# A hybrid decoder trunk: four of eight depthwise-convolution chunks as polyphase products, and a layer norm whose sums come as columns

## The chip, the cores and the metric

The kernel runs on one core of a Trainium2 chip. The metric is the device time of one execution in microseconds (us), the median of repeated runs. One execution is also recorded by the hardware profiler; its engines are PE (TensorE, the matrix engine, with its weight loads as PEld), DVE (VectorE), ACT (ScalarE), POOL (GpSimd) and SP, which here only issues transfers.

## The reference

Two layers over 512 tokens of 1024 features in float32. Layer 0 is a causal Conformer convolution, layer 1 differential attention; each is followed by a SwiGLU feed-forward network and a gated per-layer embedding. Only the convolution module is touched:

```python
def conformer_conv(x, w_pw1, b_pw1, dw_w, dw_b, ln_g, ln_b, w_pw2, b_pw2):
    a = x @ w_pw1 + b_pw1
    u = a[..., :D_MODEL] * jax.nn.sigmoid(a[..., D_MODEL:])
    u = depthwise_causal_conv(u, dw_w, width=31) + dw_b
    u = jax.nn.silu(layer_norm(u, ln_g, ln_b))     # mean and variance over the 1024 features
    return u @ w_pw2 + b_pw2
```

(The call of the convolution is shortened here; it has one filter of 31 taps for each feature.)

## The kernel before

Activations lie transposed: 128 features on the partitions and 512 tokens along a row, so that 1024 features are eight chunks. Every large product is done in three passes (`mm3`, L153) on a split of both operands into a rounded part `hi` and a rest `lo`: a weight tile of 128x1024 is loaded by SP (L146), rounded by ACT (L149), and its rest is taken by DVE (L150) or, for three tiles of the second pointwise layer, by POOL.

The convolution module runs over the eight chunks in one loop (L444 to L485). Iteration c loads the weights of chunk c+1, does the two products `half` of chunk c (gate and value, 24 matmuls each), hands the chunk before to PE's share of the convolution (`pe_taps`), gates chunk c (L462 and L467 scale, L463 is the sigmoid, L479 or L471 multiplies), finishes the chunk before (`other_taps`), and adds an earlier chunk to the running sums of the layer norm (`moments`).

The 31 taps of a chunk are shared out. In a plain chunk PE takes `PE_TAPS[c]` taps as products with diagonal matrices (L306), ACT and POOL take `POOL_TAPS[c]` (ACT multiplies, L390, POOL adds, L391), and DVE the rest, one instruction of 128x512 each (L402). DVE accumulates in a PSUM bank `sc`, except for chunk 7 (`ALONE`), where it accumulates in SBUF (`B7`) and adds PE's bank at L404; L405 adds POOL's part. A chunk in `PHASED` is done by PE alone: the gated chunk is written phase by phase (L471), stored to DRAM (`pi`, L317) and read back with four phases of 32 features on the partitions (L321). Then 4 x 9 products of 128x128x128 (L354) with matrices that hold the taps do the whole convolution. ACT copies the result (L362), it goes to DRAM (`po`, L364) and back (L367), and DVE adds the bias and orders it (L372). The nine matrix tiles of a polyphase chunk, 256 KB each, are loaded by SP into five of the six buffers `D0` to `D5` and into the two buffers of `C5`.

Before the layer norm a per-token shift, the mean over chunk 0, is taken off every chunk: by L424 for chunks below `SHIFT`, as a product of one row into PSUM (L311, L312) for later plain chunks, and inside L372 for polyphase chunks. The squares (ACT, L434) and the chunks are summed by POOL (L436, L438). For the last chunk, products with a matrix of ones put both sums on all partitions (L441, L442); eight DVE instructions (L495) read the diagonals to get them as columns, and L499 to L501 make the reciprocal deviation, which a product spreads over the partitions. `drow`, the mean, is added to all chunks (DVE L507, POOL L509), and a planned loop (L530 to L535) makes the split operands `z` of the second pointwise layer.

The order of each engine's instructions is made when the kernel is built, by a scheduler that plays the program on its own timeline; `issue_after` orders one instruction behind another, and the projections of the embedding (L524) are ordered behind the last tap or the last moment in that way. An engine's queue, SP's too, is in order.

Of the kernel before, what the change touches and what calls it, by code (L numbers as in the profile page):

```python
# [15 lines left out]
ALU = mybir.AluOpType  # L16
# [4 lines left out]
P = 128  # L21
S = 512
D = 1024
NC = D // P
# [21 lines left out]
NV = _at  # L46


SHIFT = 2
WARM = 9  # L50
ZW = 3
ALONE = (7,)
CUTS = 2


PE_TAPS = (0, 4, 0, 0, 0, 0, 0, 14)
POOL_TAPS = (9, 10, 0, 11, 0, 11, 0, 7)


PHASED = (2, 4, 6)  # L60
NPH = 4
FG = P // NPH
LAGS = (KW + NPH - 2) // NPH + 1
LEAD = LAGS - 1
TAPS = []
# [19 lines left out]
def trunk(ctx, tc, xT, pT, wts, diag, dww, vec, rel, onehot, lamv, out):  # L85
    nc = tc.nc
    V, A, G, T = nc.vector, nc.scalar, nc.gpsimd, nc.tensor
# [7 lines left out]
    def sb(shape, tag, bufs, dt=F32):  # L95
        uid[0] += 1
        return pool.tile(shape, dt, tag=tag, name=f"{tag}_{uid[0]}", bufs=bufs)
# [7 lines left out]
    tp = lambda: ps("tp", 2)  # L105
    wk = lambda dt=F32, shape=(P, S): sb(list(shape), "wk", 4, dt)
    big = lambda dt=F32, shape=(P, S): sb(list(shape), "big", 5, dt)
    f = lambda ap: ap.bitcast(F32)
# [10 lines left out]
    ident = sb([P, P], "ident", 1)  # L119
# [173 lines left out]
    def pe_taps(c):  # L293

        acc = accs[c] = sc() if c < NC - 2 else mm()
        if c in PHASED:
            return phased_taps(c, acc)
        if not PE_TAPS[c] and c < SHIFT:
            return
        for j in range(PE_TAPS[c]):  # L300
            if j % 4 == 0:
                n = min(4, PE_TAPS[c] - j)
                dg = sb([P, 4, P], f"D{TAPS.index((c, j)) % 6}", 1)
                with after_weights(c):
                    nc.sync.dma_start(dg[:, :n], diag[TAPS.index((c, j)), :, :n])
            last_tap[0] = T.matmul(  # L306
                acc, dg[:, j % 4], ups[c][:, j : j + S],
                start=(j == 0), stop=(j == PE_TAPS[c] - 1 and c < SHIFT),
            )
        if c >= SHIFT:  # L310
            T.matmul(acc, ones_r[0:1, :], shift[0], start=not PE_TAPS[c], stop=False)  # L311
            last_tap[0] = T.matmul(acc, ones_r[0:1, :], shift[1], start=False, stop=True)  # L312

    def phased_in(c, src):

        d = dram.tile([P, S], F32, tag=f"pi{c}", name=f"pi{c}")
        nc.sync.dma_start(d, src)  # L317
        xs = ups[c] = sb([P, NPH, LEAD + P], f"C{c // 2 % 2}", 2)
        G.memset(xs[:, :, :LEAD], 0.0)
        for i in range(NPH):  # L320
            nc.sync.dma_start(  # L321
                xs[i * FG : (i + 1) * FG, :, LEAD:],
                bass.AP(d.tensor, d.offset + i * P, [[S, FG], [FG * S, NPH], [1, P]]),
            )
# [34 lines left out]
    def phased_out(c):  # L359

        o = big()
        A.copy(o, accs[c])  # L362
        d = dram.tile([P, S], F32, tag=f"po{c}", name=f"po{c}")
        nc.sync.dma_start(d, o)  # L364
        both_ = sb([P, 2, S], f"B{c}", 1)
        for g in range(NPH):
            nc.sync.dma_start(  # L367
                both_[g * FG : (g + 1) * FG, 1].rearrange("p (r n) -> p r n", r=NPH),
                bass.AP(d.tensor, d.offset + g * P, [[S, FG], [FG * S, NPH], [1, P]]),
            )  # L370
        tok = "p (n r) -> p n r"
        V.scalar_tensor_tensor(  # L372
            both_[:, 0].rearrange(tok, r=NPH), both_[:, 1].rearrange("p (r n) -> p n r", r=NPH), col("dw_b", c),
            shrow.rearrange(tok, r=NPH), ALU.add, ALU.add,
        )
        y.append(both_[:, 0])

    def other_taps(c):
        if c in PHASED:
            return phased_out(c)  # L380
        up, acc = ups[c], accs[c]
        tap = lambda j: up[:, j : j + S]
        a, b = PE_TAPS[c], PE_TAPS[c] + POOL_TAPS[c]
        pacc = wk()
        for j in range(a, b):
            if j == a:
                A.activation(pacc, tap(j), AF.Identity, scale=wt(c, j), bias=col("dw_b", c))
            else:
                pr = sb([P, S], f"C{2 + j % 2}", 2)
                A.activation(pr, tap(j), AF.Copy, scale=wt(c, j))  # L390
                G.tensor_tensor(pacc, pacc, pr, ALU.add)  # L391
        yc = sb([P, 2, S], f"B{c}", 1)
        if c == 1:
            sums["acc"] = yc[:, 1]
        yc = yc[:, 0]
        alone = c in ALONE
        sum_ = yc if alone else acc
        if alone or (not a and c < SHIFT):
            V.tensor_scalar(sum_, tap(b), wt(c, b), None, ALU.mult)
            b += 1  # L400
        for j in range(b, KW):
            V.scalar_tensor_tensor(sum_, tap(j), wt(c, j), sum_, ALU.mult, ALU.add)  # L402
        if alone and a:
            V.tensor_tensor(yc, yc, acc, ALU.add)  # L404
        V.tensor_tensor(yc, sum_, pacc, ALU.add)  # L405
        y.append(yc)
# [9 lines left out]
    def moments(c):  # L416
        if c == 0:
            t = sums["first"] = tp()
            T.matmul(t, ones, y[0], start=True, stop=True)
            A.activation(shift[0], t[0:1, :], AF.Copy, scale=-1.0 / P)  # L420
            A.activation(shrow, t, AF.Copy, scale=-1.0 / P)
            V.scalar_tensor_tensor(shift[1], t[0:1, :], -1.0 / P, f(shift[0]), ALU.mult, ALU.subtract)
        if c < SHIFT:
            V.scalar_tensor_tensor(y[c], sums["first"], -1.0 / P, y[c], ALU.mult, ALU.add)  # L424
        if c < SHIFT - 1:
            return
        for i in range(SHIFT) if c == SHIFT - 1 else (c,):
            if i == NC - 1:
                sums["mean"], sums["sq"] = tp(), tp()
            if i == 0:  # L430
                A.activation(sums["acc"], y[0], AF.Square)
                continue
            sq = wk()
            A.activation(sq, y[i], AF.Square)  # L434
            if i < NC - 1:
                G.tensor_tensor(sums["acc"], sums["acc"], sq, ALU.add)  # L436
                if i > 1:
                    G.tensor_tensor(macc, y[1] if i == 2 else macc, y[i], ALU.add)  # L438
                continue
            for n, part, one in (("mean", macc, y[i]), ("sq", sums["acc"], sq)):  # L440
                T.matmul(sums[n], ones, part, start=True, stop=False)  # L441
                last_moment[0] = T.matmul(sums[n], ones, one, start=False, stop=True)  # L442

    for c in range(NC):  # L444
        wa, wg = pairs[c]
        if c == 0:
            pg = half(wg)
            norm.diagonal()
            pa = half(wa)
            rb = norm.rows()  # L450
        if c + 1 < NC:
            pairs.append((weight(), weight())[::-1])
            pair_loads.append(loaded[0])
        if c > 0:
            pg = half(wg)
            if c - 1 not in PHASED:
                pe_taps(c - 1)
            pa = half(wa)
            if c - 1 in PHASED:
                pe_taps(c - 1)  # L460
        tg, ta = big(), big()
        V.tensor_tensor(tg, pg, rb, ALU.mult)  # L462
        A.activation(tg, tg, AF.Sigmoid, bias=col("b_pw1", 8 + c))  # L463
        if c == NC - 1:

            A.activation(sb([P, 8], "lam", 1), vt[:, :8], AF.Silu)
        V.tensor_tensor(ta, pa, rb, ALU.mult)  # L467
        if c in PHASED:
            up = big()
            phases, tok = "p (r n) -> p n r", "p (n r) -> p n r"  # L470
            V.scalar_tensor_tensor(  # L471
                up.rearrange(phases, r=NPH), ta.rearrange(tok, r=NPH), col("b_pw1", c),
                tg.rearrange(tok, r=NPH), ALU.add, ALU.mult,
            )
            phased_in(c, up)
        else:
            up = ups[c] = sb([P, S + PAD], f"C{c % 2}", 2)
            G.memset(up[:, :PAD], 0.0)
            V.scalar_tensor_tensor(up[:, PAD:], ta, col("b_pw1", c), tg, ALU.add, ALU.mult)  # L479
        if c > 0:  # L480
            other_taps(c - 1)
        if c == 2:
            moments(0)
        elif c > 3:
            moments(c - 3)  # L485
# [3 lines left out]
        moments(c)  # L489

    vs = sb([P, P // 2], "v8", 2)[:, :8]
    junk = wk()
    for at, t in ((4, sums["mean"]), (0, sums["sq"])):
        for b in range(4):
            V.tensor_tensor_reduce(  # L495
                out=junk[:, b * P : (b + 1) * P], in0=t[:, b * P : (b + 1) * P], in1=ident,
                scale=1.0 / D, scalar=0.0, op0=ALU.mult, op1=ALU.add, accum_out=vs[:, at + b : at + b + 1],
            )
    V.tensor_tensor(vs[:, 4:8], vs[:, 4:8], vs[:, 4:8], ALU.mult)  # L499
    V.tensor_tensor(vs[:, 0:4], vs[:, 0:4], vs[:, 4:8], ALU.subtract)  # L500
    lrow = spread(diagonal(rsqrt_cols(vs[:, 0:4], 4, 1.0)))  # L501
# [541 lines left out]
```

## Time and profile before

| | |
|---|---|
| median of 3 runs | 1311.96 us (1311.76 to 1312.21) |
| the profiled execution | 1313.88 us, span of its trace 1312.1 us |
| PE busy | 1276.4 us, 97% |
| DVE busy | 759.3 us, 58% |
| ACT busy | 526.9 us, 40% |
| POOL busy | 276.1 us, 21% |
| mean granted PE clock | 0.988 |
| HBM read, written | 124.52 MB, 3.69 MB |

The rows that the prediction quotes are of five kinds. Slices: the span in 40 equal parts, each digit the busy tenths. Windows: a stretch in us and its length, then busy time and instruction count of PE, PEld, DVE, ACT and POOL, the granted clock, the DMA share and GB/s. Waits: who waited for whom, total us, times, longest. Timeline: start in us, length in us, engine, line, operation, tiles, count of merged instructions, and in brackets the idle time before it with what ended it. Groups: line, engine, operation, tiles, shapes, count, then busy us, mean ns, and idle time before. Where three numbers stand with slashes, they are the shortest, median and longest duration in ns. A float32 matmul that isn't split shows as two rows, one for each pass.

### The profile page before, as it was taken

The numbers are of one execution on the slowest core, as the hardware profiler recorded it, in microseconds if no ns is written. First come the engines' busy times: TensorE is split into PE (matmuls) and PEld (weight loads), VectorE is DVE, ScalarE is ACT, GpSimd is POOL, SyncE is SP. The second block draws the span as 40 slices with busy tenths as digits, with TensorE's granted clock in tenths as the row PEclk, the third lists the DMA queues.
The fourth block names the chain that finished last, engine by engine and source line by source line (L and its number), as shares of the span: only waits on it lengthen the run. The fifth ranks groups of instructions, "written<-read, shape, count | busy, mean of one in ns | idle before, by whom it ended". The sixth has DMA issues, their size and how long they took to land. (4 is left out here: it accounts for less than half of the span.)

```text
span 1312.1 us, 15285 instructions
## 1 busy us (share of the span) xinstructions
PE 1276.4 (97%) x5830; PEld 1047.4 (80%) x5830; DVE 759.3 (58%) x1168; ACT 526.9 (40%) x832; POOL 276.1 (21%) x219
## 2 busy tenths in 40 slices
PE   8999889999999999999999998999999999999998
PEld 5787668888888888888888886778888888888887
DVE  6998866544344434455678888945543344334445
ACT  5644255332123212253566767734332233223332
POOL 4839533000000000022345534122000000000030
PEclk8999889999999999999999998999999999999999
DMA  5554203332333232232222221213233323222231
GB/s 193 182 179 156 81 32 113 96 97 80 113 96 96 81 112 96 77 116 94 72 97 81 86 75 49 97 33 128 97 96 97 96 97 97 96 96 88 80 122 64
DMA packets 44534, 129.21 MB, mean 98 GB/s; under 512 B 5123, under 2 KB 8835, under 8 KB 44460
## 3 DMA queue, kind: packets, MB, share of 16 engines
q1 hardware_dynamic: 42912, 125.84, 29.2%
q10 hardware_dynamic: 1548, 2.39, 0.6%
q8 instruction: 46, 0.75, 0.2%
q14 instruction: 28, 0.23, 0.1%
HBM read 124.52 MB, written 3.69 MB: 98 GB/s over the span
## 5 line engine op out<-in xcount | busy, mean ns | idle before, releaser
L149 ACT CAST whi<-wraw 128x1024 fp32r<-128x1024 f32 (+2 forms) x214 | 218.5, 1026 | 563.5 <-PE mm L157 363.1
L155 PE MATMUL mm<-A,wlo 128*128 128x512 f32 (+1 forms) x1096 | 425.6, 392 | 9.5 <-ACT A L533 5.9
L156 PE MATMUL mm<-A,whi 128*128 128x512 f32 (+1 forms) x1096 | 428.9, 392 | 0.7 <-DVE A L170 0.5
L157 PE MATMUL mm<-A,whi 128*128 128x512 f32 (+1 forms) x1096 | 426.5, 390 | 0.0
L150 DVE TENSOR_TENSOR wlo<-wraw,whi 128x1024 fp32r<-128x1024 f32 (+2 forms) x207 | 257.5, 1248 | 66.6 <-ACT whi L149 66.2
L155 PEld LDWEIGHTS mm<-A,wlo 128*128 128x128 f32 x1096 | 207.2, 189 | 55.2 <-ACT A L533 6.7
L156 PEld LDWEIGHTS mm<-A,whi 128*128 128x128 f32 x1096 | 207.0, 189 | 48.0 <-DVE A L170 3.8
L157 PEld LDWEIGHTS mm<-A,whi 128*128 128x128 f32 x1096 | 207.0, 189 | 43.3 <-issue 1.3
L189 POOL TENSOR_TENSOR acc<-acc,wk 128x512 f32<-128x512 f32 x42 | 68.6, 1634 | 786.7 <-issue 673.3
L156 PE MATMUL mm<-B,whi 128*128 128x512 f32 x352 | 137.5, 391 | 0.0
L157 PE MATMUL mm<-B,whi 128*128 128x512 f32 x352 | 137.5, 391 | 0.0
L155 PE MATMUL mm<-B,wlo 128*128 128x512 f32 x352 | 137.1, 391 | 0.0
L591 DVE TENSOR_TENSOR h<-mm,h 128x512 f32<-128x512 f32 x48 | 33.0, 691 | 123.1 <-PE mm L157 123.0
L583 DVE TENSOR_TENSOR big<-mm,rb 128x512 f32<-128x512 f32 x44 | 30.4, 691 | 126.2 <-PE mm L157 126.2
L581 DVE TENSOR_TENSOR big<-mm,rb 128x512 f32<-128x512 f32 x44 | 30.4, 691 | 99.0 <-PE mm L157 92.6
L157 PEld LDWEIGHTS mm<-B,whi 128*128 128x128 f32 x352 | 66.1, 188 | 14.5
L156 PEld LDWEIGHTS mm<-B,whi 128*128 128x128 f32 x352 | 66.0, 188 | 14.3
L155 PEld LDWEIGHTS mm<-B,wlo 128*128 128x128 f32 x352 | 66.1, 188 | 14.2
L157 PE MATMUL mm<-whi,A 128*128 128x512 f32 x192 | 75.6, 395 | 0.0
L156 PE MATMUL mm<-wlo,A 128*128 128x512 f32 x192 | 75.0, 396 | 0.0
L155 PE MATMUL mm<-whi,A 128*128 128x512 f32 x192 | 74.8, 396 | 0.0
L214 POOL TENSOR_TENSOR r<-v,mhalf 128x8 f32<-128x8 f32 (+1 forms) x31 | 47.4, 1530 | 114.6 <-DVE v L212 92.4
(207 smaller groups left out, 1439.0 us busy)
## 6 DMA issues: line engine op xcount, KB each, us to landing
wraw<-in_wts SPq DMA_DIRECT2D x194, 512.0 KB, 3.5
wraw<-in_wts SPq DMA_DIRECT2D x16, 384.0 KB, 2.9
D<-in_diag SPq DMA_DIRECT2D x19, 256.0 KB, 4.7
C<-in_diag SPq DMA_DIRECT2D x12, 256.0 KB, 5.5
h<-in_xT SPq DMA_DIRECT2D x8, 256.0 KB, 5.3
bias<-scr ACTq DMA_DIRECT2D x8, 256.0 KB, 3.5
out_t<-h SPq DMA_DIRECT2D x7, 256.0 KB, 2.0
wraw<-in_wts SPq DMA_DIRECT2D x4, 256.0 KB, 4.8
```

The costliest lines, as they stand in the source:

```text
L149: A.copy(hi[:, cut], raw[:, cut])
L150: eng.tensor_tensor(lo[:, cut], raw[:, cut], f(hi[:, cut]), ALU.subtract)
L155: T.matmul(acc, al, bh, start=first, stop=False)
L156: T.matmul(acc, ah, bl, start=False, stop=False)
L157: return T.matmul(acc, ah, bh, start=False, stop=last)
L189: self.eng.tensor_tensor(self.acc, self.acc, sq, ALU.add)
L214: last_pow[0] = G.tensor_tensor(r[:, :n], v[:, :n], mhalf[:, :n], ALU.pow)
L581: V.tensor_tensor(tg, pg, rb, ALU.mult)
L583: V.tensor_tensor(tu, pu, rb, ALU.mult)
L591: V.tensor_tensor(h[m], acc, h[m], ALU.add)
```

## The change

Chunks 1, 3, 5 and 6 are polyphase instead of 2, 4 and 6. Chunk 1 loses its diagonal taps, chunk 7 keeps 8 of 14, and POOL's shares are set anew; DVE's shares, the rest, become 21, 20, 20 and 15 for chunks 0, 2, 4 and 7 (before: 22, 17, 20, 20 and 10 for chunks 0, 1, 3, 5 and 7). All polyphase inputs use the two buffers `C1` and all plain ones `C0`. The polyphase results are stored by ACT's queue instead of SP's. `SHIFT` falls to 1. The sums of chunks 6 and 7 no longer go through POOL: `add_moments` takes for each set four columns of squares and four of values, each from a product of one column with the data as the weights, and one wide product for the mean. The diagonal readings go away.

```diff
-SHIFT = 2
+SHIFT = 1
...
-PE_TAPS = (0, 4, 0, 0, 0, 0, 0, 14)
-POOL_TAPS = (9, 10, 0, 11, 0, 11, 0, 7)
-PHASED = (2, 4, 6)
+PE_TAPS = (0, 0, 0, 0, 0, 0, 0, 8)
+POOL_TAPS = (10, 0, 11, 0, 11, 0, 0, 8)
+PHASED = (1, 3, 5, 6)
...
-                dg = sb([P, 4, P], f"D{TAPS.index((c, j)) % 6}", 1)
+                dg = sb([P, 4, P], f"D{2 + j // 4}", 1)
...
-        xs = ups[c] = sb([P, NPH, LEAD + P], f"C{c // 2 % 2}", 2)
+        xs = ups[c] = sb([P, NPH, LEAD + P], "C1", 2)
...
-        nc.sync.dma_start(d, o)
+        nc.scalar.dma_start(d, o)
...
-        if c == 1:
+        if c == 0:
             sums["acc"] = yc[:, 1]
...
-            if i == NC - 1:
-                sums["mean"], sums["sq"] = tp(), tp()
...
-            if i < NC - 1:
+            if i < NC - 2:
                 G.tensor_tensor(sums["acc"], sums["acc"], sq, ALU.add)
                 if i > 1:
                     G.tensor_tensor(macc, y[1] if i == 2 else macc, y[i], ALU.add)
                 continue
-            for n, part, one in (("mean", macc, y[i]), ("sq", sums["acc"], sq)):
-                T.matmul(sums[n], ones, part, start=True, stop=False)
-                last_moment[0] = T.matmul(sums[n], ones, one, start=False, stop=True)
+            if i == NC - 2:
+                sums["mean"], sums["cols"] = tp(), tp()[:, 0:8]
+                add_moments(macc, sums["acc"], True, False)
+            add_moments(y[i], sq, False, i == NC - 1)
+
+    def add_moments(a, b, first, last):
+
+        for k in range(8):
+            src = (b if k < 4 else a)[:, k % 4 * P : (k % 4 + 1) * P]
+            last_moment[0] = T.matmul(sums["cols"][:, k : k + 1], src, ones[:, 0:1], start=first and k == 0, stop=last and k == 7)
+        T.matmul(sums["mean"], ones, a, start=first, stop=last)
...
-            up = ups[c] = sb([P, S + PAD], f"C{c % 2}", 2)
+            up = ups[c] = sb([P, S + PAD], "C0", 2)
...
-        if c == 2:
+        if c == 1:
             moments(0)
...
-    junk = wk()
-    for at, t in ((4, sums["mean"]), (0, sums["sq"])):
-        for b in range(4):
-            V.tensor_tensor_reduce(
-                out=junk[:, b * P : (b + 1) * P], in0=t[:, b * P : (b + 1) * P], in1=ident,
-                scale=1.0 / D, scalar=0.0, op0=ALU.mult, op1=ALU.add, accum_out=vs[:, at + b : at + b + 1],
-            )
+    V.tensor_scalar(vs, sums["cols"], 1.0 / D, None, ALU.mult)
```

## The prediction

> **What bounds the kernel now.** I read the page's forty slices first, then the busy time by stretch of the stage that the diff touches, then the waits there, then the engines' timelines.
>
> ```profile
> span 1312.1 us, 15285 instructions
> ...
> PE   8999889999999999999999998999999999999998
> ```
>
> ```profile
> 27.00:129.30 102.30, 101.06 (x496) 82.70 (x494) 92.98 (x109) 54.33 (x75) 69.49 (x48) 0.98 0.51 175
> 129.30:134.80 5.50, 0.03 (x1) 0.00 (x0) 5.29 (x9) 1.76 (x2) 2.68 (x2) 0.90 0.76 234
> 134.80:145.70 10.90, 10.83 (x73) 10.87 (x74) 8.75 (x12) 0.00 (x0) 3.37 (x4) 0.74 0.35 113
> ...
> 174.20:180.00 5.80, 0.00 (x0) 0.00 (x0) 5.80 (x7) 3.20 (x5) 5.80 (x4) 0.83 0.16 61
> 180.00:190.00 10.00, 9.92 (x33) 7.67 (x34) 9.00 (x14) 9.41 (x15) 1.23 (x2) 0.76 0.15 52
> ```
>
> TensorE (PE, first column after the length) is full from 190 us to the end, so everything the change can move lies before. In the convolution module PE and VectorE (DVE, third) are level: from 27.0 to 129.3 PE works 101.06 of 102.3 us and DVE 92.98. Then PE stands still twice, for 5.5 and 5.8 us, and after each the granted clock (third number from the end) is 0.74 to 0.76 for about ten us.
>
> ```profile
> PE mm L155 <- ACT A L533: 5.9, 1, 5.9
> PE mm L354 <- DMA C<-pi: 5.5, 1, 5.5
> ...
> DVE B L405 <- POOL wk L391: 3.1, 1, 3.1
> ```
>
> ```profile
> 142.12 0.74 DVE L479 SCALAR_TENSOR_TENSOR C<-big,vec,big 128x512 f32<-128x512 f32 x1
> 144.70 2.37 DVE L399 TENSOR_SCALAR B<-C,C 128x512 f32<-128x512 f32 x1 [1.83 <-POOL C L478]
> 147.10 8.40 DVE L402 SCALAR_TENSOR_TENSOR B<-C,C,B 128x512 f32<-128x512 f32 x6
> 155.41 1.10 DVE L372 SCALAR_TENSOR_TENSOR B<-B,vec,shrow 128x512 f32<-128x512 f32 x1
> 156.43 4.11 DVE L402 SCALAR_TENSOR_TENSOR B<-C,C,B 128x512 f32<-128x512 f32 x3
> 160.65 0.69 DVE L404 TENSOR_TENSOR B<-B,mm 128x512 f32<-128x512 f32 x1
> 164.44 0.69 DVE L405 TENSOR_TENSOR B<-B,wk 128x512 f32<-128x512 f32 x1 [3.10 <-POOL wk L391]
> ...
> 168.73 0.17 DVE L212 TENSOR_SCALAR v<-v 128x4 f32<-128x4 f32 x1
> ```
>
> The second standstill is the end of the layer norm: PE waits for the first normalised chunk. What comes last before it is DVE's chain for chunk 7: its input (L479) is written at 142.9, its ten taps, chunk 6's finish (L372) and two sums run to 165.1, of which 3.1 us wait for GpSimd (POOL), and the statistics reach L212 at 168.7. PE had finished all products of the first pointwise layer at 129.3. So chunk 7 started 13 us later than PE allowed, because DVE still owed chunk 5's taps. The end of that DVE chain sets the start of the rest.
>
> **The change part by part.** First DVE up to chunk 7's input.
>
> ```profile
> L402 DVE SCALAR_TENSOR_TENSOR sc<-C,C,sc 128x512 f32<-128x512 f32 x78 | 57.6, 750 | 1.3
> ...
> L471 DVE SCALAR_TENSOR_TENSOR big<-big,vec,big 128x512 f32<-128x512 f32 x3 | 5.6, 1875 | 0.3 <-ACT big L463 0.3
> L372 DVE SCALAR_TENSOR_TENSOR B<-B,vec,shrow 128x512 f32<-128x512 f32 x2 | 4.3, 2130 | 0.5 <-DMA B<-po 0.5
> L479 DVE SCALAR_TENSOR_TENSOR C<-big,vec,big 128x512 f32<-128x512 f32 x5 | 4.2, 845 | 0.8 <-ACT big L463 0.8
> L405 DVE TENSOR_TENSOR B<-sc,wk 128x512 f32<-128x512 f32 x4 | 2.8, 689 | 0.3
> L424 DVE SCALAR_TENSOR_TENSOR B<-tp,B 128x512 f32<-128x512 f32 x2 | 1.4, 677 | 0.0
> ```
>
> These are DVE's groups from 35.3 to 142.9. Chunks 0, 1, 3, 5 give it 22+17+20+20 = 79 taps; after, chunks 0, 2, 4 give 21+20+20 = 61. That is 18 x 0.75 = 13.5 us less, about 12.6 since neighbouring rows overlap by 0.05. One more permuted input is +1.9 (L471), one plain input, one sum and one shift fewer are -0.85 (L479), -0.69 (L405) and -0.68 (L424), and one more polyphase finish in this stretch (chunks 1, 3, 5 against 2, 4) is +2.1 (L372). Together -10.8, and with DVE's short waits left as they are it could write chunk 7's input at 132.
>
> Now PE over the same stretch.
>
> ```profile
> 48.48 3.60 PE L306 MATMUL sc<-C,D 128*128 128x512 f32 x8
> 51.51 0.79 PE L155 MATMUL mm<-A,wlo 128*128 128x512 f32 x1
> ...
> 73.02 1.02 PE L419 MATMUL tp<-B,ones 128*128 128x512 f32 x2
> 73.88 4.18 PE L354 MATMUL sc<-C,D 128*128 128x128 f32 x36
> ...
> 81.83 0.48 PE L155 MATMUL mm<-A,wlo 128*128 128x512 f32 x1
> ...
> 145.67 12.18 PE L306 MATMUL mm<-C,D 128*128 128x512 f32 x28
> 157.78 0.50 PE L311 MATMUL mm<-bias,ones 1*128 1x512 f32 x1
> ...
> 158.44 0.51 PE L155 MATMUL mm<-wth,wlo 128*128 128x512 f32 x1
> ```
>
> A polyphase chunk is 73.88 to 81.83 = 7.95 us. Chunk 1's four diagonal taps are 48.48 to 51.51 = 3.03, and a plain fp32 product of 512 columns (two passes) is 73.88 - 73.02 = 0.86. Up to the last pointwise product PE gets three polyphase chunks (1, 3, 5) for two (2, 4) and loses chunk 1's taps: +7.95 - 3.03 = +4.9. Shift rows are as many as before, six (two each for chunks 2, 4, 7, not 3, 5, 7). So PE ends the pointwise products at 129.3 + 4.9 = 134.2, after DVE's 132: PE sets chunk 7's input, and L467 (0.68) and L479 (0.74) put it at 135.7. I add 0.5 for one more handover of a polyphase chunk to PE: 136.2, against 142.9.
>
> Chunk 7's own chain then grows: PE takes 8 of its taps, not 14, and POOL 8, not 7, so DVE has 15, not 10. Its taps run from SBUF to SBUF beside POOL's additions.
>
> ```profile
> L402 DVE SCALAR_TENSOR_TENSOR B<-C,C,B x9: 740/1641/1789, 147.1 to 158.9; 128x512 f32<-128x512 f32 x9
> ...
> L391 POOL TENSOR_TENSOR wk<-wk,C x43: 1268/1299/2272, 36.9 to 163.1; 128x512 f32<-128x512 f32 x43
> ...
> 156.59 1.70 POOL L438 TENSOR_TENSOR acc<-acc,B 128x512 f32<-128x512 f32 x1 [2.44 <-DVE B L372]
> ```
>
> A tap takes 0.74 alone and 1.64 beside POOL, whose addition goes from 1.30 to 1.70. The bounds for 15 taps plus L372, plus 1.4 for the two sums: 16 x 0.75 + 0.4 + 1.4 = 13.8 us with no meeting, 16 x 1.64 + 0.5 + 1.4 = 28.1 with one at each. POOL has 7 additions for chunk 7 (the first tap is ScalarE's) and perhaps one left over from chunk 5, since the change takes chunk 6's two additions away from POOL. So I take 8 meetings: 8 x 1.64 + 8 x 0.75 + 0.4 + 1.4 = 20.9. POOL itself ends near 136.2 + 1.5 + 8 x 1.70 = 151.3, so L405's 3.1 us wait goes. Chunk 7 is complete at 136.2 + 20.9 = 157.1, not 165.1: -8.0. The Trainium skill, "SBUF — State Buffer", section "Who interferes with whom", holds that a DVE instruction with two SBUF inputs and a GpSimd instruction that reads SBUF exclude each other, the later one waiting the whole time. By that rule a tap that arrives just behind an addition costs 1.30 + 0.74 = 2.0 and not 1.64, the same sum gives 24, and the gain shrinks to about 5 us; the trace's 1.64 and 1.70, on both sides together, look like such turns with part of the wait already over.
>
> The statistics.
>
> ```profile
> 22.66 1.05 PE L195 MATMUL tp<-ones,acc 128*128 128x1 f32 x8
> ...
> 166.52 0.29 DVE L495 CUSTOM_DVE_ANT_0 wk<-tp,ident 128x128 f32<-128x128 f32 x1 [1.39 <-PE tp L442]
> ...
> 168.53 0.16 DVE L500 TENSOR_TENSOR v<-v 128x4 f32<-128x4 f32 x1
> ```
>
> The eight diagonal readings (166.52 to 168.5) become one small DVE instruction of 0.2. But between the last square and it now stand eight one-column products: four (eight passes) start over 0.92 us at L195, so eight take 1.84, with 0.25 for the last to end, where 0.86 stood. From chunk 7 complete to L212 I get 0.04 + 0.63 (square) + 0.1 + 1.84 + 0.25 + 0.05 + 3 x 0.2 = 3.5 against 168.73 - 165.13 = 3.6: nothing. From L212 to the first normalised chunk I take the same 11.3 us.
>
> Is PE in time? After 134.2 it owes 7.95 (chunk 6), 8 x 0.86 = 6.9, shift 0.66, two sets of eight columns and two mean products 2 x (1.84 + 0.86) = 5.4: 155.1, before chunk 7's square at 157.8. The projections that fill gaps (L157 `wth`) can slip behind. If they don't, PE is about 1 us late. In total PE works 4.0 us more: +7.95 for the fourth polyphase chunk, -10 x 0.86 for the diagonal taps, +5.5 for 24 columns, -0.86 for one wide product. That takes the place of the 5.5 us standstill and of the 2.9 us lost in the slow clock behind it (10.9 for a block of 7.95).
>
> The queues. SP gets 38 matrix loads for 32, one more polyphase input (five issues) and four more reads back, about 15 x 0.45 = 6.8 us of issuing; it loses the four stores to ScalarE, on which it waited:
>
> ```profile
> SPq L364 <- ACT big L362: 12.9, 3, 5.1
> ...
> 70.56 0.56 ACTq L636 DMA_DIRECT2D C<-in_onehot  x1
> ```
>
> ScalarE pays 4 x 0.56 us, behind copies for which it waits in any case, and is busy 54 of 102 us. I cost this at nothing. If that cover is gone, weight loads come late and PE waits: that is the slower rival.
>
> Sum: -8.0 us. The profiled execution took 1313.88 (span 1312.1), so it becomes 1305.9; against the median 1311.96, which lies 1.9 lower, 1304.0.
>
> **The rivals.** *The lock eats it.* POOL's additions, the moments' and the moved weight splits spread so that each DVE tap meets one: 28.1, chunk 7 complete at 164.3, -0.8: 1311.2. For it: L402's median is 1.64, so most of the nine rows met one. Against it: POOL loses work. The true point may lie between this and the forecast.
>
> *PE never cools.* If chunk 7 comes earliest, PE sets the pace: columns start at 155.1 in place of 157.8, and the standstill at the layer norm shrinks, since more PE work than before is left to fill it. Ten us at clock 0.76 cost 2.4 us; without them -8.0 - 2.4 = 1301.6, with the earlier columns too 1298.9. The Trainium skill, "TensorE: Matmul & The Clock Gate", section "Part 1: The HAM clock gate", says the clock halves after an idle window of some 3.4 us. By that rule a standstill of 3 us would be free of it, and the trace agrees as far as it goes: both standstills here are 5.5 us or longer and both are followed by a low clock.
>
> *PE stalls between pointwise products.* Chunk 1's round trip through DRAM comes when only chunk 2's and 3's products can cover it, and chunk 6's matrices wait for buffers that chunk 5's taps hold. A wait like the one for `pi` costs 5.5 + 2.9 = 8.4 us, and before it cost little, as no pointwise product stood behind it. One such wait puts chunk 7's input at 144.6, and the total at 1312.4; two give 1320.8. It decides from 10.6 us of added standstill before 134 us. For it: DVE's slack on PE is only 2 us, and SP carries more. Against: the polyphase chunks 2 and 4 show no wait on `pi`, and PE has other products to take first.
>
> **How the numbers follow.** A measurement tells about 0.2%, 2.6 us, from no change. I give 0.54 to the forecast (its own range 1302 to 1308), 0.12 to PE that never cools, 0.15 to the lock, 0.19 to the stalls. Faster 0.66, same 0.15, slower 0.19. The range reaches from 1299 (PE's floor) to 1316 (half way into the stalls).
>
> **What would show it.** Right: chunk 7's L479 ends near 136, chunk 7 complete near 157, no PE standstill before it over 2 us, L212 3.5 us after chunk 7 is complete, first pointwise-2 product near 172. Wrong: PE below 97% between 27 and 134 us; L402 into `B` with 15 rows of 1.6 or more; PE's columns starting late because taps or moments of chunk 6 are; a low clock at another place.

## The result and the profile after

The changed kernel takes 1319.44 us (median of six runs, 1316.7 to 1321.83), the kernel before on the same chip 1312.11: a ratio of 1.0052, 95% interval 1.0038 to 1.0066. It is slower by 7 us where 8 us less were forecast. The profiled execution is the fastest of the six, 1316.7 us with a span of 1314.9, so its trace shows 2.8 us of the loss (1312.1 before). What the other runs have on top has no trace and stays open.

Windows of the changed kernel: the stretch and its length, then busy time (and instructions) of PE, PEld, DVE, ACT and POOL, the granted clock, the DMA share and GB/s.

```profile
27.00:129.30 102.30, 102.30 (x547) 86.87 (x546) 89.23 (x105) 49.64 (x68) 56.66 (x41) 0.98 0.61 198
129.30:134.80 5.50, 5.50 (x39) 5.06 (x38) 0.00 (x0) 1.51 (x2) 2.31 (x1) 1.00 0.69 240
134.80:145.70 10.90, 10.90 (x61) 7.69 (x60) 8.93 (x7) 5.13 (x9) 7.83 (x5) 1.00 0.42 139
...
150.00:162.00 12.00, 0.47 (x1) 0.00 (x0) 11.68 (x11) 0.00 (x0) 5.62 (x4) 0.51 0.04 12
162.00:174.20 12.20, 12.01 (x41) 9.62 (x42) 3.45 (x10) 1.86 (x3) 1.66 (x2) 0.51 0.00 0
...
162.00:185.00 23.00, 22.81 (x86) 18.16 (x87) 9.23 (x15) 8.76 (x13) 12.08 (x8) 0.74 0.02 2
```

From 27 to 150 us the change does on PE what it was expected to do: PE is full, the standstill of 5.5 us before chunk 6's polyphase products is gone, and from 129.3 on the clock is 1.00. Then PE stands still for nearly 12 us and comes back at half clock (0.51 until 174.2). The waits say on what:

```profile
PE tp L448 <- DVE B L372: 11.7, 1, 11.7
...
DVE B L372 <- DMA B<-po: 9.3, 1, 9.3
...
DVE v L498 <- PE tp L447: 7.4, 1, 7.4
```

DVE's timeline (start, length, line, operation, tiles) has the first and the last of these. L372 finishes a polyphase chunk; L473 and L485 write chunk 7's input, L399 and L402 are its taps, L498 takes the sums:

```profile
136.53 1.12 DVE L372 SCALAR_TENSOR_TENSOR B<-B,vec,shrow 128x512 f32<-128x512 f32 x1 [9.27 <-DMA B<-po]
137.57 0.68 DVE L473 TENSOR_TENSOR big<-mm,rb 128x512 f32<-128x512 f32 x1
138.35 1.27 DVE L485 SCALAR_TENSOR_TENSOR C<-big,vec,big 128x512 f32<-128x512 f32 x1
139.66 2.48 DVE L399 TENSOR_SCALAR B<-C,C 128x512 f32<-128x512 f32 x1
142.17 18.96 DVE L402 SCALAR_TENSOR_TENSOR B<-C,C,B 128x512 f32<-128x512 f32 x14
161.04 1.09 DVE L372 SCALAR_TENSOR_TENSOR B<-B,vec,shrow 128x512 f32<-128x512 f32 x1
...
162.83 0.69 DVE L405 TENSOR_TENSOR B<-B,wk 128x512 f32<-128x512 f32 x1
170.92 0.17 DVE L498 TENSOR_SCALAR v<-tp 128x8 f32<-128x8 f32 x1 [7.40 <-PE tp L447]
...
171.51 0.17 DVE L212 TENSOR_SCALAR v<-v 128x4 f32<-128x4 f32 x1
```

PE's timeline has the middle one. L447 is a column product, L448 the wide product for the mean; eight rows are four products of two passes:

```profile
147.46 1.05 PE L447 MATMUL tp<-ones,B 128*128 128x1 f32 x8
148.38 1.03 PE L447 MATMUL tp<-ones,acc 128*128 128x1 f32 x8
149.27 1.20 PE L448 MATMUL tp<-acc,ones 128*128 128x512 f32 x2
162.19 2.08 PE L448 MATMUL tp<-B,ones 128*128 128x512 f32 x2 [11.72 <-DVE B L372]
164.06 1.71 PE L447 MATMUL tp<-ones,wk 128*128 128x1 f32 x8
...
171.81 1.42 PE L155 MATMUL mm<-wth,wlo 128*128 128x512 f32 x1
...
185.11 0.39 PE L155 MATMUL mm<-A,wlo 128*128 128x512 f32 x1
```

Three things are to be seen. Chunk 5's finish stands at the head of DVE's queue and waits 9.27 us for its read back, with chunk 7's input behind it. Chunk 6's finish stands behind all fifteen taps of chunk 7, and PE's next instruction, chunk 6's mean product, waits for it, with projections queued behind (e2 below shows three of them to be ready). And the columns, 1.05 us for eight passes at 147, take 1.71 and more when PE returns. The clock had begun to fall right behind the first of them: it is 0.96 from 147.4 to 150.4 and 0.50 from there. L212 comes at 171.5 (before 168.7), the first product of the second pointwise layer at 185.1 (before 180.1). PE doesn't wait for the norm then, as it is still at the projections; before, it waited:

```profile
180.08 2.13 PE L155 MATMUL mm<-A,wlo 128*128 128x512 f32 x4 [5.92 <-ACT A L533]
```

The trace of the first wait, from the timelines of ACT's and SP's queues (SP's four matrix loads and the read back; ACT's store):

```profile
126.56 1.80 SPq L340 DMA_DIRECT2D C<-in_diag  x4
...
133.09 1.75 SPq L367 DMA_DIRECT2D B<-po  x4
```

```profile
127.69 0.35 ACTq L364 DMA_DIRECT2D po<-big  x1
```

What the transfers issued from 118 to 136 us took to land (count, KB each, median us), and then the same over all stores and reads back of `po` in before:

```profile
D<-in_diag SPq DMA_DIRECT2D x6, 256.0 KB, 4.1
...
C<-in_diag SPq DMA_DIRECT2D x4, 256.0 KB, 4.9
...
po<-big ACTq DMA_DIRECT2D x1, 256.0 KB, 5.4
```

```profile
DMA to landing us min/median/max: 1.8/1.9/2.7
```

The store of 5.4 us is chunk 5's, from 127.69 to the read back at 133.09; L372 follows 3.4 us later. Five of chunk 6's nine matrices, 256 KB each, were issued between 124.8 and 128.4, and the DMA share is 0.69 in the second window above. The other three stores on that queue, of chunks 1, 3 and 6, landed in 2.3, 4.2 and 2.0.

### The profile page after: what moved, and what is told of

It is laid out like the page before. It is cut to its first block, busy times and chain, and to the rows that moved or that the text cites. A ratio compares the mean times of both kernels' runs of the same rounds, so it can differ in the third digit from the quotient of the medians.

```text
span 1314.9 us, 15447 instructions
## 1 busy us (share of the span) xinstructions
PE 1281.4 (97%) x5928; PEld 1057.4 (80%) x5928; DVE 748.3 (57%) x1139; ACT 522.8 (40%) x825; POOL 261.4 (20%) x210
```

## The experiments

Lines of after are named; where an edit moves them, a quoted row has the kernel's own. Ratios are to the kernel before, on the same chip, with their 95% interval.

| run | what it is | us | ratio |
|---|---|---|---|
| e1_order6 | after, chunk 6's finish earlier | 1319.07 | 1.0041 (1.0023 to 1.0059) |
| e2_wide | after, sums as before | 1316.38 | 1.0022 (1.0011 to 1.0033) |
| e3_cols | before, sums as columns | 1315.30 | 1.0011 (1.0000 to 1.0021) |
| e4_defer5 | after, chunk 5's finish later | 1316.57 | 1.0025 (1.0012 to 1.0039) |
| e5_wide64_before | e3 with 64 columns | 1310.78 | 0.9973 (0.9963 to 0.9984) |
| e6_wide64 | after with 64 columns | 1319.25 | 1.0038 (1.0024 to 1.0051) |
| e7_split | after, chunk 7 shared as before | 1314.37 | 1.0007 (0.9997 to 1.0016) |
| e8_all | 64 columns, both finishes, projections first | 1310.90 | 0.9982 (0.9971 to 0.9993) |
| e9_best | 64 columns, both finishes, chunk 7 as before | 1305.11 | 0.9936 (0.9918 to 0.9953) |
| e10_split64 | e7 with 64 columns | 1310.07 | 0.9969 (0.9958 to 0.9980) |
| e11_all_narrow | e8 with one column | 1311.99 | 0.9985 (0.9974 to 0.9996) |
| e12_best_fill | e9 with projections first | 1311.64 | 0.9981 (0.9968 to 0.9994) |

The edits below are shown in part; `late` holds the finishes that are put off. The theory at first was that the two finishes on DVE's queue are the cause: PE stands still for them and cools. The rival was that the columns are. The first four runs take one part each.

**e1_order6**: the last six DVE taps of chunk 7 are ordered behind chunk 6's finish.

```diff
-        V.scalar_tensor_tensor(
+        fin[c] = V.scalar_tensor_tensor(
...
         for j in range(b, KW):
+            if c == NC - 1 and j >= KW - 6:
+                with tc.issue_after(fin[6].ins):
+                    V.scalar_tensor_tensor(sum_, tap(j), wt(c, j), sum_, ALU.mult, ALU.add)
+                continue
```

> The changed kernel, with chunk 7's last six DVE taps ordered behind chunk 6's finish (L372), nothing else. Theory Q (chunk 6's finish stands behind chunk 7's 14 taps on DVE, PE's queue stands still on chunk 6's mean product for 11.7 us and cools to half clock): chunk 6 is complete near 154 instead of 162, PE's wait for it falls from 11.7 to about 5 us, the statistics (L212) come near 167.5 instead of 171.5, and the time falls by about 4 us, to 1315. Rival C (the one-column products are the cost): 24 of them still stand on the path, the time stays within 1 us of 1319. Rival S (what matters is that chunk 7's input came late, behind chunk 5's finish): also no change, since that input stays at 139.

DVE's and PE's timelines of this run:

```profile
157.09 1.08 DVE L374 SCALAR_TENSOR_TENSOR B<-B,vec,shrow 128x512 f32<-128x512 f32 x1
```

```profile
158.89 1.87 PE L453 MATMUL tp<-ones,wk 128*128 128x1 f32 x8 [7.79 <-ACT wk L438]
...
163.39 1.42 PE L155 MATMUL mm<-wth,wlo 128*128 128x512 f32 x1
```

The finish comes 4 us earlier and PE's standstill shrinks by 4, to 7.79, but no gain can be told (1.0041 against 1.0052, the intervals overlap). The eight taps ahead of the finish take 14.23 us beside POOL, as they do in after; only the six fast ones have moved behind it. PE comes back as cold as before (eight passes in 1.87), and spends 163.4 to 169.4 on projections before chunk 7's columns. The place of that finish isn't enough by itself.

**e2_wide**: after, with the layer norm's sums taken as before.

```diff
...
-            if i == NC - 2:
-                sums["mean"], sums["cols"] = tp(), tp()[:, 0:8]
-                add_moments(macc, sums["acc"], True, False)
-            add_moments(y[i], sq, False, i == NC - 1)
+            for n, part, one in (("mean", macc, y[i]), ("sq", sums["acc"], sq)):
+                T.matmul(sums[n], ones, part, start=True, stop=False)
+                last_moment[0] = T.matmul(sums[n], ones, one, start=False, stop=True)
...
```

> The changed kernel with the layer norm's sums done as before (POOL adds chunk 6, four wide products, eight diagonal readings); all else of the change stays. Rival C: 24 one-column products less on a cold PE, 1312 or lower. Theory Q: chunk 6 is still complete only at 162, POOL's two additions for it (1.3 to 1.7 us each) come after that, and PE, if its queue has the projections in front, no longer stands on chunk 6; the wait moves to POOL, L212 near 169 to 171, the time 1315 to 1319.

PE's timeline, the first projection and the end of its longest wait:

```profile
147.40 0.50 PE L155 MATMUL mm<-wth,wlo 128*128 128x512 f32 x1
...
162.00 0.80 PE L155 MATMUL mm<-wth,wlo 128*128 128x512 f32 x1 [10.26 <-DVE B L404]
```

The standstill is there without any column: what PE waits for is now chunk 7 itself. The mean product of chunk 6 is no longer at the head of PE's queue, so three projections go first, from 147.4 to 151.7; the fourth needs one of the four `mm` banks of PSUM, and waits until L404 has read chunk 7's. So three were ready, some 4 us of work. The clock is 0.50 from 160 to 165. By the ratios 4 us of the 7 are gone. As the edit changes this order too, the columns are at most a part of the loss.

**e3_cols**: before, with the columns alone (`add_moments`, and L498 for the eight diagonal readings; chunks and taps as before).

```diff
...
-            for n, part, one in (("mean", macc, y[i]), ("sq", sums["acc"], sq)):
-                T.matmul(sums[n], ones, part, start=True, stop=False)
-                last_moment[0] = T.matmul(sums[n], ones, one, start=False, stop=True)
+            if i == NC - 2:
+                sums["mean"], sums["cols"] = tp(), tp()[:, 0:8]
+                add_moments(macc, sums["acc"], True, False)
+            add_moments(y[i], sq, False, i == NC - 1)
...
```

> The kernel before with only the column sums put in (add_moments, one small DVE instruction in place of the eight diagonal readings). Theory Q: in the kernel before, PE is busy with chunk 7's 14 diagonal taps until 157.8 and chunk 6 is complete at 156.5, so PE does not stand on it and stays warm; the columns cost nothing on the path: 1312, within 1.5 us. Rival C: plus 3 us or more, 1315 to 1317.

Its windows over the columns, which begin at 157.98:

```profile
158.40:159.40 1.00, 1.00 (x11) 1.00 (x10) 1.00 (x1) 0.00 (x0) 0.55 (x1) 1.00 0.00 0
159.40:160.40 1.00, 1.00 (x5) 0.62 (x5) 0.79 (x3) 0.00 (x0) 0.00 (x0) 0.72 0.00 0
160.40:162.00 1.60, 1.60 (x6) 0.95 (x4) 0.69 (x1) 0.63 (x1) 0.00 (x0) 0.50 0.00 0
...
164.00:172.00 8.00, 8.00 (x25) 5.90 (x26) 0.80 (x5) 0.07 (x1) 1.03 (x1) 0.50 0.01 2
```

With e5 below, this decides what the columns do. PE is busy in every microsecond, and yet the granted clock is at 0.50 two us after the first column and stays there to 172. The Trainium skill, "TensorE: Matmul & The Clock Gate", section "Part 1: The HAM clock gate", says that the gate follows how busy the array has been over a window of about 3.4 us; the trace agrees only if a product of one column hardly counts as busy, which the page doesn't say and no row here shows directly. From chunk 7 complete (161.1) to L212 (170.55) it takes 9.5 us, 3.6 before. As chunk 7 is complete 4 us earlier in this trace, the time rises by only 1.4 us, by the ratio.

**e4_defer5**: after, chunk 5's finish ordered behind chunk 7's input.

```diff
...
-            V.scalar_tensor_tensor(up[:, PAD:], ta, col("b_pw1", c), tg, ALU.add, ALU.mult)
+            gated = V.scalar_tensor_tensor(up[:, PAD:], ta, col("b_pw1", c), tg, ALU.add, ALU.mult)
+            if late:
+                with tc.issue_after(gated.ins):
+                    late.pop()()
```

> The changed kernel, with chunk 5's finish (L372) ordered behind chunk 7's input on DVE instead of ahead of its scaling L473. Rival S: chunk 7's input comes 6 us earlier (at 133.5, PE had its products ready at 131.8), everything after it moves by as much, 1313 to 1314. Theory Q: chunk 7's taps start 6 us earlier but chunk 6's finish still stands behind them; its data land at 152, so with 14 taps ending at 155 chunk 6 is complete near 156, PE's wait shrinks from 11.7 to about 6 us: 1314 to 1316. If neither is right it stays at 1319.

DVE's timeline:

```profile
133.89 0.76 DVE L493 SCALAR_TENSOR_TENSOR C<-big,vec,big 128x512 f32<-128x512 f32 x1
138.61 1.12 DVE L375 SCALAR_TENSOR_TENSOR B<-B,vec,shrow 128x512 f32<-128x512 f32 x1 [3.96 <-DMA B<-po]
139.65 0.48 DVE L407 TENSOR_SCALAR B<-C,C 128x512 f32<-128x512 f32 x1
```

Chunk 7's input ends at 134.7, 5 us earlier, but the scheduler puts the finish straight behind it, and DVE waits again. Chunk 7 is complete at 162.5 instead of 163.5; PE's standstill is 9.5. By the ratios it brings 3.5 us of the 7, with intervals that just touch; its trace doesn't show where (span 1314.8, L212 at 172.3). The first tap takes 0.48 here; it took 2.48 in after, where POOL's weight split of 2.83 us had begun at 139.02. The thirteen taps behind it take 19.05, though, about as long as fourteen in after.

The new theory: PE is cold through the layer norm for two causes, the one-column products and the standstill, and either alone is enough. Its test is to take away one, the other, and both.

**e5_wide64_before**: e3, each column product 64 equal columns wide, L498 reading every 64th.

```diff
...
-sums["cols"][:, k : k + 1], src, ones[:, 0:1]
+sums["cols"][:, k * 64 : (k + 1) * 64], src, ones[:, 0:64]
...
```

> The kernel before with the column sums, as in e3_cols, but each product is 64 columns wide (the same matrix of ones, 64 equal columns) and the small DVE instruction reads one of 64. Theory H (one-column products leave the array idle, so the granted clock falls to 0.5 while PE is busy, as in e3_cols from 159.7 on): 64 columns keep the clock up, eight products take 1.8 to 2.0 us and not 3.4, L212 comes near 164 to 166 instead of 170.6, and the time falls from 1315.3 to 1311 or lower. Rival C (24 more products with their weight loads cost time as such): no gain against e3_cols, 1315. If the products' width itself costs, later still.

Two of the windows shown for e3, and a row of columns on PE:

```profile
159.40:160.40 1.00, 1.00 (x11) 1.00 (x11) 0.93 (x3) 0.00 (x0) 0.00 (x0) 1.00 0.00 0
...
164.00:172.00 8.00, 8.00 (x43) 6.56 (x43) 4.63 (x8) 2.58 (x5) 4.26 (x3) 1.00 0.01 2
```

```profile
162.02 1.06 PE L447 MATMUL tp<-ones,B 128*128 128x64 f32 x8
```

The clock is 1.00 throughout, and a product of 64 columns costs what one column cost warm: 1.06 us for eight passes against 1.03 to 1.05. Nothing else was changed, and by the ratios the time falls by 5 us, below that of before.

**e6_wide64**: the same edit on after.

> The changed kernel with 64-column products in place of one-column ones. Theory H: the first set no longer brings the clock down at 150, but PE then waits 11.7 us for chunk 6 with nothing to do, so the clock falls all the same and the second and third set still start cold: a gain of 0 to 2 us, 1317.5 to 1319.5. Theory Q alone (the wait cools PE, width does not matter): no change, 1319. If the one-column width alone were the whole loss: 1314 or lower.

PE's timeline:

```profile
164.17 2.08 PE L448 MATMUL tp<-B,ones 128*128 128x512 f32 x2 [9.54 <-DVE B L372]
166.03 1.81 PE L447 MATMUL tp<-ones,wk 128*128 128x64 f32 x8
```

No gain that can be told (1319.25). The columns no longer cool PE, but the standstill of 9.54 us does: the wide columns behind it take 1.81 too.

**e7_split**: after, chunk 7's taps shared as before, 14 on PE, 7 on ACT and POOL, 10 on DVE.

```diff
-PE_TAPS = (0, 0, 0, 0, 0, 0, 0, 8)
-POOL_TAPS = (10, 0, 11, 0, 11, 0, 0, 8)
+PE_TAPS = (0, 0, 0, 0, 0, 0, 0, 14)
+POOL_TAPS = (10, 0, 11, 0, 11, 0, 0, 7)
```

> The changed kernel with chunk 7's taps shared out as before: 14 on PE, 7 on POOL, 10 on DVE. The price of the new split by itself. If chunk 7's longer DVE list is what delays it: DVE's chain is 5 taps of 1.35 to 1.64 shorter, chunk 7 complete near 156 instead of 163.5, 1312 or lower. Theory H: PE's diagonal taps now end at 152, all 24 one-column products come after them, and they take about 15 us with the means at half clock whatever DVE does: L212 near 167 to 168, 1315 to 1316.

PE's timeline, chunk 6's first columns:

```profile
157.99 1.86 PE L447 MATMUL tp<-ones,wk 128*128 128x1 f32 x8 [1.69 <-ACT wk L432]
```

The six taps given back cost PE 5.1 us, all of which falls where it stood still: the wait is 1.69 in place of 11.7, chunk 7 is complete at 158.7, and the time falls to that of before. The edit has two sides, more work for PE and five taps fewer for DVE, and no run parts them. What is left is the cold of the one-column products (1.86): the clock is already 0.51 from 155 on. With 64 columns it is **e10_split64**:

> The changed kernel with two edits: chunk 7 shared out as before, and 64-column products. e7_split had the first alone (1314.4), e6_wide64 the second alone (1319.3, nothing gained). Theory H: with PE warm up to the columns the width now counts, L212 falls from 167.3 to about 163, 1310 to 1311. If width counts nothing here, as in e6_wide64: 1314.

PE's timeline, around the same place:

```profile
155.33 1.08 PE L448 MATMUL tp<-acc,ones 128*128 128x512 f32 x2
158.62 1.97 PE L447 MATMUL tp<-ones,wk 128*128 128x64 f32 x8 [2.21 <-ACT wk L432]
...
165.44 1.06 PE L447 MATMUL tp<-ones,B 128*128 128x64 f32 x8
```

The time is right, 1310.07, but won in another place than expected: behind a wait of 2.21 us the clock was at one half from 158.5 to 165.4, so L212 comes at 167.1 as in e7. What the width saves lies behind it: PE is warm again some 6 us earlier, and the first product comes at 179.1, not 181.9.

**e9_best**: e10, with chunk 5's finish behind the fourth DVE tap of chunk 7 and the last two taps behind chunk 6's finish. It beats both kernels.

```diff
...
         for j in range(b, KW):
-            V.scalar_tensor_tensor(sum_, tap(j), wt(c, j), sum_, ALU.mult, ALU.add)
+            if late and c == NC - 1 and j in (b + 3, KW - 2):
+                with tc.issue_after(did.ins):
+                    late.pop(0)()
+                did = fin[6 if j == KW - 2 else 5]
+            if c == NC - 1 and j > b:
+                with tc.issue_after(did.ins):
+                    did = V.scalar_tensor_tensor(sum_, tap(j), wt(c, j), sum_, ALU.mult, ALU.add)
+                continue
+            did = V.scalar_tensor_tensor(sum_, tap(j), wt(c, j), sum_, ALU.mult, ALU.add)
```

> The changed kernel with 64-column products, chunk 7 shared out as before (14 taps on PE, 7 on POOL, 10 on DVE), chunk 5's finish behind chunk 7's fourth DVE tap and the last two taps behind chunk 6's finish. Theory H with Q: PE has diagonal taps until 152 and so no standstill ahead of chunk 6's moments, the columns run at full clock, chunk 7 is complete near 155, L212 comes near 161 to 163, and what PE has left fills the layer norm better: 1306 to 1309, ratio 0.995 to 0.998. If PE's six more diagonal taps are themselves too dear: 1311 or higher.

Its windows over the norm:

```profile
155.00:160.00 5.00, 5.00 (x37) 4.25 (x36) 2.35 (x4) 0.63 (x1) 0.00 (x0) 1.00 0.00 2
160.00:165.00 5.00, 5.00 (x28) 3.80 (x27) 1.22 (x5) 0.76 (x2) 1.61 (x2) 1.00 0.00 0
165.00:170.00 5.00, 5.00 (x22) 3.81 (x21) 5.00 (x4) 2.68 (x5) 5.00 (x4) 1.00 0.00 0
170.00:175.00 5.00, 5.00 (x23) 4.11 (x23) 4.32 (x5) 4.77 (x8) 4.94 (x4) 1.00 0.00 0
```

PE neither stands still nor cools, here and in the windows beside these. Chunk 7's input ends at 136.2 and chunk 7 at 158.0 (155 was expected), L212 is at 163.1, and the first product at 175.1. The gain is a little larger than expected (0.9936, not 0.995 to 0.998). That 136.2 and 158.0 lie near the prediction's 136.2 and 157.1 is chance: it had fifteen DVE taps between them, and this kernel has ten.

**e8_all**, **e11_all_narrow** and **e12_best_fill** fill PE in another way: three projections (m = 0 to 2) are put ahead of the moments of chunks 6 and 7. e8 is after with that, 64 columns and both finishes moved as in e9 (behind the sixth tap, and before the last three); e11 is e8 with one column; e12 is e9 with those projections.

```diff
...
+    for m in range(3):
+        with tc.issue_after(last_tap[0].ins):
+            pp.append(project(ph, m, w, sb([P, S], f"D{m}", 1)))
+    with tc.issue_after(last_pp[0].ins):
+        for c in range(NC - 2, NC):
+            moments(c)
...
```

> The changed kernel with all the supposed mends together: 64-column products, three of the embedding's projections placed on PE ahead of chunk 6's moments, chunk 5's finish behind the sixth tap of chunk 7, chunk 7's last three taps behind chunk 6's finish. Theories H and Q together (PE must stay warm through the layer norm and must not stand on chunk 6): chunk 7's input at 134.6, chunk 7 complete near 158, PE without a standstill over 3 us until then, L212 near 162 to 164 (1311.96's kernel: 168.7), the time 1305 to 1308, under both kernels. If the loss is of another kind: 1314 or higher.

> The kernel of e8_all with its products one column wide again, nothing else. Theory H: the clock falls to 0.5 in the course of the columns although PE has projections on both sides, L212 comes at 164.5 to 167 instead of 162.9, and the time goes from 1310.9 to 1313 to 1315. If the order of the work was all that counted: 1311.

> As e9_best, with three projections placed on PE ahead of chunk 6's moments as in e8_all. By H and Q, PE has no standstill in front of those moments in e9_best already, so the three projections (4.1 us) only push the columns back: L212 2 us or so later than in e9_best, but less is left to do afterwards than the layer norm hides: within 2 us of e9_best, on the slower side, 1307 to 1310.

PE's timeline of e8, the first product of the second pointwise layer:

```profile
174.50 2.07 PE L155 MATMUL mm<-A,wlo 128*128 128x512 f32 x4 [3.60 <-ACT A L556]
```

e8 takes 1310.9, not the expected 1305 to 1308. It has L212 at 162.9, as early as e9, and is still 6 us slower: the projections that were spent early are missing while the norm is computed, PE runs dry for 3.60 us before its first product, and the clock is 0.52 from 175 to 180. e12 repeats this on e9: the same wait of 3.60, and 6.5 us lost where at most 2 were expected. In e11 the columns are cold again (clock 0.50 from 160 to 165), but the expected further loss did not come: 0.9985 against e8's 0.9982, intervals overlapping. The slower columns move projections into the later gap, which shrinks to 2.40 and is followed by clock 1.00. So one cause of cold PE can hide another.

## Why the prediction was wrong

What held: with 18 taps fewer DVE was done with chunk 4 at 124.9, and PE ended the pointwise products at 131.8 (134.2 forecast) without a standstill; four round trips and 38 matrices never stopped it before 150, so the rival of stalls between pointwise products is false in its place. The diagonal readings for columns came out at nothing with PE warm: in e5 from chunk 7 complete (162.7) to L212 (166.4) 3.7 us, forecast 3.5.

What failed, along the prediction's own path:

- **"The queues ... I cost this at nothing."** The cover was gone at one place. The store of `po` for chunk 5, moved to ACT's queue, landed 5.4 us after its issue, and L372, which waits for it, stands ahead of chunk 7's input on DVE. Input at 139.6, not 136.2: +3.4. What made the store slow wasn't tried; that SP's loads took 4.1 to 4.9 us in the same stretch, and chunk 6's store on the same queue 2.0, speaks for the traffic rather than the queue. By its ratio e4, which moves this wait, is 3.5 us faster, but its trace doesn't show the gain.
- **"So I take 8 meetings."** From input to chunk 7 complete it took 23.9 us, not 20.9: +3.0. The count was right: of the fourteen rows of L402 eight take 1.63 to 2.08 us, from 142.2 to 156.4 beside POOL, and six take 0.75. The prices were not: the first tap took 2.48 beside POOL's weight split where 0.75 was put (+1.7), though the prediction's own row of before has 2.37; two of the eight took 2.08 (+0.9); the gaps between the rows are the rest. The sum by the rule of the Trainium skill, "SBUF — State Buffer", section "Who interferes with whom", was 24. The trace agrees in total, but by luck: six of the eight meetings cost 1.63 to 1.65 and not 2.0, and the dear first tap makes up for it.
- **"Is PE in time?"** This is the step that failed and decides. It counted PE's work at full clock, took every operand as ready, and put PE at most about 1 us late. In order, PE stood behind chunk 6's mean product, and chunk 6's finish, whose read back was issued from 148.2 on and needs some 2 us to land, stood behind fifteen taps until 161.0: a standstill of 11.7 us, ended 1.3 us before chunk 7 was complete. The standstill of 5.5 us that it took as removed went, and so did that of 5.9 us at the norm; one of 11.7 took their place. The signs of being wrong name this ("PE's columns starting late because taps or moments of chunk 6 are; a low clock at another place"), but no term of the sum and no rival has a price for it.
- **"The statistics ... nothing."** 163.5 to 171.5 is 8.0 us, not 3.5: +4.5. The columns were priced from a row at full clock; cold, eight passes take 1.71 to 1.85.
- From L212 to the first product 13.6 us against 11.3: +2.3. The product that spreads the deviation (L229) stands behind projections, the first of them cold, and starts at 178.5, 7.0 us after L212; before it started 4.3 after, and it began as soon as its operand (L219) was there. Here that operand had been there for 5 us.

The sum is -8.0 + 3.4 + 3.0 + 4.5 + 2.3 = +5.2 for the first product; it is 5.0 later. Part of this comes back, because PE has worked at projections meanwhile. PE's own account is nearer to the span: +0.3 of standstill (11.7 for 5.5 + 5.9), +4.0 of work as forecast, +0.7 of slow clock (the last window, 23 us at 0.74, loses 6.0, where the prediction counted 2.9 + 2.4 for before), -1.2 of idle time between 27 and 129.3: +3.8, where the trace shows +2.8; the last microsecond isn't resolved. The change took DVE off the path and paid PE for it, but PE got none of its cold time back.

In the same account e9 has neither standstill, no slow clock, 5.1 us more work for six more taps, and 0.7 more idle time between 27 and 129.3 (PE works 100.36 of the 102.3 us): -11.4 - 5.3 + 4.0 + 5.1 + 0.7 = -6.9, against -6.5 by its span (1305.6). This is what the rival "PE never cools" stood for, though in a kernel with the old split, 64 columns and another order; the rival had overlooked the one-column products. What the theory says of after is shown by the pairs: by the ratios width gains 5 us where the columns run without a long standstill (e3 to e5, e7 to e10) and 2 at most on after (e6, the intervals overlap); the split alone gains 6, and split, width and order together 15 (1.0052 to 0.9936).

## What to carry to other kernels

An engine that runs in order needs a look at each instruction that waits, and at what is queued behind it: DVE's L372 ahead of chunk 7's input held DVE for 9.3 us, and PE's mean product, ahead of three projections that were ready, held PE for 11.7. Where the clock follows PE's activity, price a product by its row at the clock that it will meet, make products of a few columns wider if that is free, and close all gaps of a stage, since one cause of cold PE hides another. Keep PE's spare work for the stretch in which everything else is slow: the same three projections were worth 6.5 us behind the sums rather than ahead of them.

## What was not expected of the hardware

A busy PE row says nothing of the clock: with one-column float32 products back to back it fell from 1.00 to 0.50 within 2 us (e3), and with 64 columns, at the same time for a pass, it stayed at 1.00 (e5). Gaps of 3.54 to 3.60 us (e1, e8, e12) were followed by a slow clock, gaps of 1.82 and 2.40 (e8, e11) weren't, and one of 2.21 behind 64-column products and a wide one was (e10); so 64 columns may not count in full either, which no run here settles. Nor do one-column products always cool PE: chunk 7's set in e1, between projections (169.4 to 171.1), ran at 1.00, and so did what came behind it.
